# One pass for bias and maximum, zero-padded queries, and a searched order of the attention work

## Chip, cores and metric

The kernel runs on one core of a Trainium2 chip. The metric is the device time of one execution, in microseconds (us), as the median of three runs. All engine names are those of the profile: PE is the matrix engine, DVE, ACT and POOL are the vector, scalar and GpSimd engines, SP issues most DMAs.

## The reference

Two transformer layers act on 384 tokens: 256 latent tokens (a grid of 4 rows by 64 columns) and 128 context tokens. A layer normalises and modulates the tokens, projects them with one matrix, runs three kinds of attention on column groups of the result, concatenates their outputs, projects them, and adds a gated feed-forward network. All data are float32. The attention that the change touches is the neighbourhood kind, with 6 heads of width 64:

```
s_win = einsum('bhrqd,bhrjkd->bhrqjk', qg, kg) * scale + bias     # all 4 grid rows
s_win = where(in_win, s_win, NEG)                                 # 16 columns around the query
s_ctx = einsum('bhrqd,bhcd->bhrqc', qg, k_ctx) * scale            # 128 cached context keys
p = softmax(concatenate([s_win, s_ctx]))
o = p_win @ v + p_ctx @ v_ctx
```

The others are latent attention (MLA, 6 heads with keys of width 96) and differential attention (4 heads, the difference of two softmax maps). Context tokens attend to context tokens alone, in all three kinds.

## The kernel before

Tokens are handled in three tiles of 128 (two latent, one context). Every large product is split into a high and a low float32r part, so each product of 128 rows is three matmuls (`mm3`, lines 321 to 323). The weights arrive by DMA in `raw`, ACT rounds them to `wh` (line 254), and DVE forms the rest `wl` (line 260).

A layer has three stages. First comes the input projection, cut into 72 units of six matmuls (`g1`, tiles `z<-wh,hh`). I call them dense units, since PE can run them back to back. Second is attention, in pieces that are interleaved with the dense units. Third are the output projection and the feed-forward network. The output projection has 8 output blocks `m` of 8 units (three matmuls each, tiles `z<-oxh,wh` and `z<-o,wh`); the first three blocks are begun inside the attention stage.

The order of everything in the first two stages is made by a planner (`Plan`) when the program is built. Each piece is a task with an engine, a length in us, a priority, predecessors and the buffers it takes. `Plan.order` simulates the engines, always starts the ready task of lowest priority value, and lists the tasks by their simulated start. The program is recorded in that order, so every engine has one fixed queue. The planner halves PE's speed in windows that follow a thinly filled one. From the fourth output block on, the tile scheduler places instructions.

A softmax piece (`soft`) is: scores on PE (`score`, line 1037), the negated maximum on DVE (`maxima`, 1045), exponentials on ACT (`exps`, 1056), reciprocal and scaling on DVE (`norm`, 1061 and 1066), transposes of the weights on PE (`blocks_T`, 1004), and their copy on ACT (1106). `pair` makes four such pieces of 128 latent queries by 384 keys (two heads, two tiles), one piece for the context tokens, and the product with the values (1139, 1142). Neighbourhood pairs are made by `near(0)`, `near(1)` and `near(2)`, differential heads by `diff(0)` to `diff(3)`; `ORDER` lists in which sequence their priorities rise.

Before the change the two heads of a neighbourhood pair lie in partitions 0 to 63 and 64 to 127 of one tile, so a score matmul has 64 rows. The bias of 256 latent keys is added in place (line 1100) before the maximum is taken over 384. The bias tile has 6 x 64 columns. Normalised queries and keys come out of PE transposes (line 1209); ACT copies the queries (1212), DVE the keys (1215). `done_n` holds these steps.

Of the kernel before, what the change touches and what calls it, by code (L numbers as in the profile page):

```python
# [11 lines left out]
F32 = mybir.dt.float32  # L12
F32R = mybir.dt.float32r
AF = mybir.ActivationFunctionType
ALU = mybir.AluOpType
# [35 lines left out]
WARMUP = (18, 0.43, 16)  # L51
CYCLE = 'zszstzt'
# [5 lines left out]
HOPS = {('pe', 'act'): 0.2, ('pe', 'dve'): 0.16, ('act', 'pe'): 0.22, ('dve', 'pe'): 0.27, ('pool', 'dve'): 0.06, ('act', 'dve'): 0.15, ('dve', 'act'): 0.15}  # L58
# [23 lines left out]
class Plan:  # L82
# [8 lines left out]
    def add(self, eng, dur, fn, after=(), take=(), frees=(), prio=0.0, ready=0.0):  # L91
        t = Task(eng, dur, fn, take, prio, ready, LAG if eng == 'dma' else 0.0)
        self.tasks.append(t)
        for a in after:
            if a is not None:
                a.then.append(t)
                t.need += 1
        for h in frees:
            h.users += 1
            t.frees.append(h)  # L100
        return t

# [80 lines left out]
def trunk(ctx: ExitStack, tc, xT_d, cv_d, crow_d, pcol_d, prow_d, cache_d, dfk_d, rope_d, bias_d, ident_d,  # L183
# [378 lines left out]
    def parameters(l, staged=None):  # L562
# [14 lines left out]
        naq, lam, nlam, subg = (par.tile([P, 1], F32, tag=t, name=nm(t)) for t in ("naq", "lam", "nlam", "subg"))  # L577
# [7 lines left out]
        def gains():  # L585
            nc.vector.tensor_scalar(prow[:, PR_DQ:PR_DQ + 32], prow[:, PR_DQ:PR_DQ + 32], 32.0 ** -0.5, None, op0=ALU.mult)
            nc.vector.tensor_scalar(naq, pc[:, PC_NAQ:PC_NAQ + 1], 0.125, None, op0=ALU.mult)
# [25 lines left out]
    for l in range(DEPTH):  # L613
# [177 lines left out]
        def g1(ci, done, kbs=(0, 2, 4, 6), kind="z"):  # L791
# [3 lines left out]
            for kb in kbs:  # L795
# [3 lines left out]
                for t in range(3):  # L799
# [7 lines left out]
                    u = add(PE, 6 * (n / 2400 + 0.003), unit, after=[lo, last[t], hready[kb], hready[kb + 1]],  # L807
# [95 lines left out]
        def up_q(t, pr):  # L903
# [37 lines left out]
            p = add(POOL, 1.6, lambda: rsqrt(x["rs"], x["ms"], 96 * EPS), after=red, prio=pr)  # L941
# [5 lines left out]
        def up_kv(i, pr):  # L947
# [34 lines left out]
            p = add(POOL, 1.6, lambda: rsqrt(x["rs"], x["ms"], mskr[:, i:i + 1]), after=red, prio=pr)  # L982
# [38 lines left out]
        def soft(maps, after, spread, bias=None, joint=None, keep=None):  # L1021
# [18 lines left out]
            def maxima():  # L1040
                if bias:
                    bias(x["b"][0][0])
                x["mx"], i = small(n), 0
# [4 lines left out]
            def exps():  # L1048
                x["su"], x["e"] = small(n), []
                for ps, c in x["b"]:  # L1050
                    for j in range(c):
                        i = len(x["e"])
                        if nk == NT or i == 0:
# [3 lines left out]
                                             accum_out=x["su"][:, i:i + 1])  # L1057
# [14 lines left out]
            a = add(PE, COST_S * w / NT * (0.25 if joint else 1), score, after=after, take=("s",) * banks, prio=pr + PRS)  # L1072
            b = add(DVE, 0.08 * banks + 1.05e-3 * w + (0.34 if bias else 0), maxima, after=[a], prio=pr + PRM)
# [11 lines left out]
        def pair(kt, qk, v, h0, biased, after, vals, late=None):  # L1085
# [3 lines left out]
            for i in range(2) if biased else ():  # L1089
                def fetch(i=i):  # L1090
                    p["bias", i] = wk.tile([P, 6, 64], F32, tag="bias", name=nm("bias"))
                    nc.sync.dma_start(p["bias", i], bias_d[l, :, h0 + i])
                ld[i] = add(DMA, 0.3, fetch, take=("bias",), prio=seq[0])
                in_line("bias", ld[i])
            vs, scored, rooms = [], [], []
            for i in range(2):
                for t in range(2):
                    def bias(ps, i=i, t=t):
                        u0 = 2 - 2 * t
                        nc.vector.tensor_tensor(ps[:, 0, P:NT], ps[:, 0, P:NT],  # L1100
                                                p["bias", i][:, u0:u0 + 4, :].rearrange("p u c -> p (u c)"), op=ALU.add)
# [15 lines left out]
                    else:  # L1117
# [4 lines left out]

            x, a, e, pr = soft(lambda: [(qk()[0][i][:, NL:NT], qk()[1][i][:, NT:512], i == 0 or biased) for i in range(2)], after,
                               (P, 2, 2 if biased else 1), keep="pd")
# [44 lines left out]
        nu, na_ready, na_room = [], [[] for _ in range(3)], []  # L1169
        vn, vn_ready = [], [[] for _ in range(3)]  # L1170

        def na_units():
            nu.extend(units(3, P))
            dma.dma_start(nu[1][:, :, 0:P], cache_d[l, :, CA_NAK:CA_NAK + 384].rearrange("p (a b) -> p a b", a=3))

        def done_n(j):
            hd = slice(2 * j, 2 * j + 2)

            def done(t, z, unit, room):
# [6 lines left out]
                def vals():  # L1186
                    if j < 2 and t == 0:

                        vn.append(ws.tile([P, 4, 2 + 2 * j, 64], F32, tag="v" if j else "v0", name=f"vn{l}{j}"))
                        dma.dma_start(vn[j][:, 0].rearrange("p h d -> p (h d)"),  # L1190
                                      cache_d[l, :, CA_NAV + P * j:CA_NAV + P * j + P * (1 + j)])
                    v = vn[min(j, 1)][:, :, slice(0, 2) if j < 2 else slice(2, 4)]
# [18 lines left out]
                def queries():  # L1211
                    nc.scalar.activation(nu[0][:, j, t * P:(t + 1) * P], x["pt"][:, 0], AF.Copy, scale=naq)
# [16 lines left out]
                na_ready[j].append(add(ACT, 0.26, queries, after=[f], frees=[f], prio=pr))  # L1229
# [4 lines left out]
        dfo, vd, df_ready, vd_ready = [], [], [{}, {}], [[], []]  # L1234

        def done_d(p):
            hd = slice(2 * p, 2 * p + 2)

            def done(t, z, unit, room):
# [18 lines left out]
                def rotate():  # L1258
                    if t == 0:
                        dfo.append(ws.tile([P, 3, 8, 32], F32, name=nm("dfo")))  # L1260
# [24 lines left out]
                d = add(POOL, 1.9, lambda: rsqrt(x["rs"], x["ms"], EPS), after=[c], prio=pr)  # L1285
                e = add(DVE, 0.33, lambda: nc.vector.tensor_tensor(heads(x["n"], 8), heads(x["n"], 8), bc3(x["rs"], 32), op=ALU.mult),
                        after=[d], prio=pr)
                df_ready[p][t] = add(DVE, 1.25 if t < 2 else 0.34, rotate, after=[e], frees=[a], prio=pr)
# [4 lines left out]
        def df_unit(h, after, pr):  # L1293
# [19 lines left out]
            for t in range(3):  # L1313
# [29 lines left out]
                d = add(POOL, 0.86, parts_lo, after=[c], prio=pr)  # L1343
                e = add(PE, 0.37, stack, after=[d], take=("t",), frees=[c], prio=pr)
# [7 lines left out]
        def diff_step(h, t, st, after, late=()):  # L1352
# [30 lines left out]
            o = add(PE, 0.6 if t < 2 else 0.16, out, after=[v] + vd_ready[h // 2], take=("t",), frees=[x["room"]], prio=pr + PRO)  # L1383
# [3 lines left out]
        def diff_tail(h, st, late, pr):  # L1387
# [23 lines left out]
            c = add(POOL, 1.0, lambda: rsqrt(st["rs"], st["ms"], EPS), after=[b], prio=pr)  # L1411
# [41 lines left out]
        def near(j):  # L1453
            if not dense:
                dense.extend(t for t in plan.tasks if t.dense)
            sl = [slice(64 * i, 64 * i + 64) for i in range(2)]
# [277 lines left out]
```

## Time and profile before

| what | value |
|---|---|
| median of three runs | 1035.77 us (1035.76 to 1036.49) |
| the profiled execution, its own time | 1036.13 us |
| its span in the trace | 1034.4 us |
| PE busy | 1012.3 us, 98% |
| DVE, ACT, POOL busy | 719.5, 509.1, 172.7 us |
| layer 0: first score, last value product ends, output projection ends | 98.7, 213.9, 245.4 us |
| layer 1: the same | 598.7, 723.4, 749.4 us |

The span runs from the first to the last instruction; 1.7 us of the execution lie around it. "PE busy" counts a matmul until its modelled end, so neighbours overlap and a busy PE may still be waiting between starts. The starts of successive rows of the timeline tell its pace. "PEld" is the loading of weights, and "PEclk" the share of the full clock that PE was granted.

### The profile page before, as it was taken

How to read it: one execution, taken by the hardware profiler on the slowest of the kernel's cores; microseconds unless marked ns; L12 is line 12 of the kernel's file. 1: busy time of each engine (PE TensorE's matmuls, PEld its weight loads, DVE VectorE, ACT ScalarE, POOL GpSimd, SP SyncE). 2: the span in 40 equal slices, each digit the busy share in tenths (PEclk: the TensorE clock that was granted, in tenths of full speed). 3: DMA queues.
4: the chain of work that ended last, by engine and by line, in shares of the span. 5: the costliest groups of instructions: out<-in, count | busy, mean ns of one | idle time of the engine just before them, and what ended most of it. 6: DMA issues, size and time to landing. Idle time of an engine off the chain costs nothing.

```text
span 1034.4 us, 16528 instructions
## 1 busy us (share of the span) xinstructions
PE 1012.3 (98%) x6074; PEld 933.0 (90%) x6074; DVE 719.5 (70%) x1599; ACT 509.1 (49%) x1180; POOL 172.7 (17%) x263
## 2 busy tenths in 40 slices
PE   8999999989999999999999999989999999999998
PEld 7877779679999999999978878867999999999998
DVE  5677787955999999963455887766869755554332
ACT  3466778745433333343326668766653334333221
POOL 2266223201001001100024533230010000000000
PEclk9999999989999999999999999969999999999999
DMA  9865444125575757684463232410376434343441
GB/s 356 331 202 190 161 153 138 58 82 202 165 243 185 233 177 232 206 273 131 123 226 101 81 125 71 154 54 9 123 249 199 125 120 137 108 123 111 139 137 42
DMA packets 129681, 162.25 MB, mean 157 GB/s; under 512 B 5056, under 2 KB 111680, under 8 KB 127296
## 3 DMA queue, kind: packets, MB, share of 16 engines
q1 hardware_dynamic: 121184, 132.76, 40.3%
q0 software_dynamic: 6832, 27.77, 7.7%
q8 instruction: 48, 0.79, 0.3%
q10 hardware_dynamic: 1584, 0.66, 0.2%
q14 instruction: 33, 0.27, 0.1%
HBM read 158.12 MB, written 3.05 MB: 156 GB/s over the span
## 4 chain that ended last, share of the span: by engine, by line
PE 76%; DVE 2%; ACT 1%; POOL 1%; issue 1%; ACTq 0%; DVEq 0%; POOLq 0%
PE z L321 11%; PE z L323 11%; PE z L322 11%; PE t L322 6%; PE t L321 6%; PE t L323 6%; PE s L322 5%; PE s L323 5%; PE s L321 5%; PE s L1037 2%; PE t L1004 2%; PE t L1139 1%; POOL small L542 1%; PE t L1376 1%; PE z L1037 1%
## 5 line engine op out<-in xcount | busy, mean ns | idle before, releaser
L254 ACT ACTIVATE wh<-raw 128x1024 fp32r<-128x1024 f32 (+2 forms) x216 | 201.5, 934 | 366.0 <-PE z L322 138.8
L260 DVE TENSOR_TENSOR wl<-raw,wh 128x1024 fp32r<-128x1024 f32 (+2 forms) x216 | 230.7, 1070 | 111.6 <-ACT wh L254 111.2
L321 PE MATMUL z<-fh,wh 128*128 128x386 f32 x304 | 103.2, 339 | 0.0
L322 PE MATMUL z<-fl,wh 128*128 128x386 f32 x304 | 103.0, 339 | 0.0
L323 PE MATMUL z<-fh,wl 128*128 128x386 f32 x304 | 102.6, 338 | 0.0
L444 DVE CUSTOM_DVE_ANT_0 sums<-wt,sums,pcol 128x1024 f32<-128x1024 f32 x80 | 102.2, 1278 | 0.3 <-DVE small L1578 0.3
L321 PE MATMUL z<-wh,hh 128*128 128x384 f32 (+1 forms) x264 | 99.9, 379 | 1.1 <-ACT hh L514 0.5
L323 PE MATMUL z<-wh,hl 128*128 128x384 f32 (+1 forms) x264 | 90.3, 342 | 0.5 <-DVE hl L522 0.5
L322 PE MATMUL z<-wl,hh 128*128 128x384 f32 (+1 forms) x264 | 89.8, 340 | 0.0
L542 POOL TENSOR_TENSOR small<-small,mhalf 128x4 f32<-128x4 f32 (+4 forms) x58 | 73.2, 1262 | 4.8
L321 PE MATMUL s<-fh,wh 128*128 128x386 f32 x200 | 68.2, 341 | 0.0
L321 PE MATMUL t<-fh,wh 128*128 128x386 f32 x200 | 68.1, 340 | 0.0
L322 PE MATMUL t<-fl,wh 128*128 128x386 f32 x200 | 67.8, 339 | 0.0
L322 PE MATMUL s<-fl,wh 128*128 128x386 f32 x200 | 67.8, 339 | 0.0
L323 PE MATMUL t<-fh,wl 128*128 128x386 f32 x200 | 67.5, 338 | 0.0
L323 PE MATMUL s<-fh,wl 128*128 128x386 f32 x200 | 67.5, 338 | 0.0
L438 POOL DMA_DIRECT2D wt<-in_w_modT x40 | 21.5, 539 | 273.7 <-DVE mod L444 190.8
L321 PEld LDWEIGHTS z<-wh,hh 128*128 128x128 f32 x264 | 49.8, 189 | 9.2 <-issue 4.2
L322 PEld LDWEIGHTS z<-fl,wh 128*128 128x128 f32 x304 | 57.5, 189 | 0.0
L323 PEld LDWEIGHTS z<-fh,wl 128*128 128x128 f32 x304 | 57.3, 188 | 0.0
L321 PEld LDWEIGHTS z<-fh,wh 128*128 128x128 f32 x304 | 57.2, 188 | 0.0
L1056 ACT ACTIVATE e<-s,small 128x384 f32<-128x384 f32 (+1 forms) x102 | 51.0, 506 | 12.2 <-DVE small L1045 11.2
(316 smaller groups left out, 2422.8 us busy)
## 6 DMA issues: line engine op xcount, KB each, us to landing
raw<-in_w_gate SPq DMA_DIRECT2D x22, 1024.0 KB, 6.0
raw<-in_w_up SPq DMA_DIRECT2D x22, 1024.0 KB, 5.4
raw<-in_w_down SPq DMA_DIRECT2D x32, 704.0 KB, 4.8
wt<-in_w_modT POOLq DMA_DIRECT2D x40, 512.0 KB, 4.3
raw<-in_w_mod SPq DMA_DIRECT2D x16, 1024.0 KB, 5.0
raw<-in_w_in SPq DMA_DIRECT2D x40, 384.0 KB, 3.9
raw<-in_w_out SPq DMA_DIRECT2D x8, 1024.0 KB, 5.5
qu<-in_w_mod SPq DMA_DIRECT2D x8, 512.0 KB, 7.4
```

The source lines that it names most:

```text
L254: nc.scalar.activation(hi, src, AF.Copy)
L260: nc.vector.tensor_tensor(lo, src, hi.bitcast(F32), op=ALU.subtract)
L321: nc.tensor.matmul(out, sh, mh, start=first, stop=False)
L322: nc.tensor.matmul(out, sh, ml, start=False, stop=False)
L323: nc.tensor.matmul(out, sl, mh, start=False, stop=last)
L438: nc.gpsimd.dma_start(self.w[:, self.loaded % 3], w_modT[l, c * P:(c + 1) * P])
L444: nc.vector.tensor_tensor_reduce(self.junk, self.w[:, self.n % 3], self.s[:, v], 1.0, pcol[l][:, PC_BMOD + c:PC_BMOD + c + 1], ALU.mult, A ...
L542: nc.gpsimd.tensor_tensor(out, t[:, :n], mhalf[:, :n], op=ALU.pow)
L1004: nc.tensor.transpose(pt[:, b, :], x, ident)
L1037: nc.tensor.matmul(ps[:, i, :], q, k, start=True, stop=True)
L1056: nc.scalar.activation(x["e"][i], ps[:, j, :], AF.Exp, bias=x["mx"][:, i:i + 1], accum_out=x["su"][:, i:i + 1])
L1139: nc.tensor.matmul(po[64 * i:64 * i + 64, 0:NL], vv[:, b, v0 + i, :], p["pT"][i][:, b, :], start=(b == 0), stop=(b == 2), tile_position=(0 ...
```

## The change

Neighbourhood scores: each head's query tile now has 128 rows, with zeros in the other head's 64 (the two columns of `naq` hold the gain in one half and zero in the other). ACT therefore writes two query copies for each transpose, and the score matmul uses the whole key tile. There are four query tiles, so pair 2 reuses those of pair 0, and the turning of pair 2 waits for the scores of pair 0. The two context maps now share one PSUM bank and one reduction.

Bias and maximum: one `tensor_tensor_reduce` over all 384 keys adds the bias, negates, and keeps the minimum; the exponential gets `scale=-1`. The bias tile grows to 5 x 128 columns (zeros for the context keys), the DMA from 0.20 to 0.33 MB for each of 12 loads.

Order: several task lengths and hand-over times are set anew, and `Plan.best` runs the planner 300 more times with a seeded random change of some priorities, keeping the shortest simulated order. This happens while the program is built. Tiles that were made by the first pair in program order are now made by whichever comes first.

```diff
+ORDERS, STIR = 300, 3.0
...
+    def best(self):
...
+        draw = random.Random(0)
+        base = [t.prio for t in tasks]
+        free = [i for i, t in enumerate(tasks) if t.dur and t.eng != "room"]
+        best = list(base)
+        run(best)
+        end = self.end
+        for _ in range(ORDERS):
+            p = list(best)
+            for i in draw.sample(free, draw.choice((1, 2, 4, 8, 16, 40))):
+                p[i] = base[i] + draw.gauss(0, STIR if draw.random() < 0.8 else 5 * STIR)
+            try:
+                run(p)
+            except AssertionError:
+                continue
+            if self.end <= end:
+                end, best = self.end, p
+        return run(best)
...
-HOPS = {('pe', 'act'): 0.2, ('pe', 'dve'): 0.16, ...}
+HOPS = {('pe', 'act'): 0.22, ('pe', 'dve'): 0.22, ..., ('dve', 'pool'): 0.18, ...}
-u = add(PE, 6 * (n / 2400 + 0.003), unit, ...)
+u = add(PE, 6 * (n / 2400 + 0.0135), unit, ...)
-p = add(POOL, 1.6, lambda: rsqrt(...), ...)
+p = add(POOL, 2.1, lambda: rsqrt(...), ...)
...
 def maxima():
+    x["mx"], i = small(n), 0
     if bias:
-        bias(x["b"][0][0])
-    x["mx"], i = small(n), 0
+        s = x["b"][0][0][:, 0, :]
+        s = s.rearrange("p (b k) -> p b k", k=P)
+        nc.vector.tensor_tensor_reduce(s, s, bias(), -1.0, 3e38, ALU.add, ALU.min, x["mx"])
+        return
...
-p["bias", i] = wk.tile([P, 6, 64], F32, tag="bias", name=nm("bias"))
+p["bias", i] = wk.tile([P, 5, P], F32, tag="bias", name=nm("bias"))
-x, a, e, pr = soft(... i == 0 or biased) for i in range(2)], after, (P, 2, 2 if biased else 1), keep="pd")
+x, a, e, pr = soft(... i == 0) for i in range(2)], after, (P, 2, 1), keep="pd")
...
 def queries():
-    nc.scalar.activation(nu[0][:, j, t * P:(t + 1) * P], x["pt"][:, 0], AF.Copy, scale=naq)
+    for i in range(2):
+        nc.scalar.activation(nu[0][(2 * j + i) % 4][:, t * P:(t + 1) * P], x["pt"][:, 0], AF.Copy, scale=naq[:, i:i + 1])
...
-work = plan.order()
+work = plan.best()
```

The order moves on every engine. Three places follow, each as the program before has it and then as the changed one has it.

PE in layer 1, from just after the last dense unit (`z<-wh,hh`). Lines 1037 and 1073 are the scores, 1004 and 1040 the transposes, 1376 and 1420 the value products of differential attention, 1209 and 1250 the turning of neighbourhood queries and keys, 1335 the stacking of differential queries and keys; `ku_7098` is the last differential head, `ku_7112` and `ku_6845` the neighbourhood keys.

```order
L1004 MATMUL t_7761<-ident,e_7709 128x128
L1376 MATMUL t_7768<-vd_6337,pd_7749 128x64 x3
L1037 MATMUL z_7778<-ku_7098,qu_7097 128x128 x2
L1376 MATMUL t_7793<-vd_6337,pd_7781 128x64
L1209 MATMUL t_7799<-ident,tok_7720 128x128 x2
L1037 MATMUL s_7806<-ku_7112,qu_7111 128x128
L1037 MATMUL s_7808<-ku_7112,qu_7111 128x128
L1209 MATMUL t_7823<-ident,tok_7736 128x128 x2
L1037 MATMUL z_7835<-ku_7112,qu_7111 128x384
L1004 MATMUL t_7843<-ident,e_7789 128x128 x3
L1209 MATMUL t_7859<-ident,tok_7763 128x128 x2
L1037 MATMUL z_7862<-ku_7112,qu_7111 128x384
```

```order
L1040 MATMUL t_7978<-ident,dn_7351 128x128 x3
L1040 MATMUL t_7989<-ident,e_7932 128x128 x3
L1073 MATMUL z_7999<-ku_6845,qu_6844 128x384
L1073 MATMUL z_8007<-ku_6845,qn_6846 128x384
L1073 MATMUL z_8017<-ku_6845,qn_6846 128x384
L1420 MATMUL t_8031<-vd_6345,pd_8019 128x64 x3
L1250 MATMUL t_8037<-ident,tok_7943 128x128 x2
L1073 MATMUL s_8046<-ku_6845,qu_6844 128x128
L1073 MATMUL s_8046<-ku_6845,qn_6846 128x128
L1250 MATMUL z_8050<-ident,tok_7951 128x128 x2
L1250 MATMUL t_8063<-ident,tok_7985 128x128 x2
L352 MATMUL z_8070<-oxh_5867,wh_7898 128x384
```

What follows the last dense unit before is the rest of two differential heads and all three neighbourhood pairs: 24 score rows, 45 transposes and 12 stackings up to the last value product. Now it is the rest of pair 1 and pair 2: 11 score rows, 32 transposes and no stacking, with output units (line 352) reached sooner. In layer 0 the scores fall from 20 to 10 and the transposes from 38 to 28. The dense units that stand behind the first score rise from 31 to 36 in layer 0 and from 33 to 40 in layer 1; the output units left after the last value product rise from 47 to 52 and from 49 to 51.

DVE in layer 0, from the end of attention into the output projection. `xT<-z` (534, 565) adds a finished output block, `fl` (529, 560) prepares the feed-forward input, `sq` (464, 495) sums squares, and the `wl` of line 260 or 291 is the low part that output block 3 needs.

```order
L1551 TENSOR_TENSOR fl_3058<-mod_101,fh_3057 128x8x2
L534 SCALAR_TENSOR_TENSOR xT<-z_2741,mod_101,xT 128x256
L534 SCALAR_TENSOR_TENSOR xT<-z_2741,mod_101,xT 128x128
L534 SCALAR_TENSOR_TENSOR xT<-z_2791,mod_101,xT 128x256
L534 SCALAR_TENSOR_TENSOR xT<-z_2791,mod_101,xT 128x128
L534 SCALAR_TENSOR_TENSOR xT<-z_2986,mod_101,xT 128x256
L534 SCALAR_TENSOR_TENSOR xT<-z_2986,mod_101,xT 128x128
L529 SCALAR_TENSOR_TENSOR fl_3058<-xT,aff_103,fh_3057 128x256
L529 SCALAR_TENSOR_TENSOR fl_3058<-xT,aff_103,fh_3057 128x128
L529 SCALAR_TENSOR_TENSOR fl_3058<-xT,aff_103,fh_3057 128x256
L464 TENSOR_TENSOR sq_3039<-sq_3039,sq_3043 128x384
L260 TENSOR_TENSOR wl_3048<-raw_2342,wh_3030 128x1024
```

```order
L1598 TENSOR_TENSOR fl_3052<-mod_101,fh_3051 128x8x2
L565 SCALAR_TENSOR_TENSOR xT<-z_2779,mod_101,xT 128x256
L565 SCALAR_TENSOR_TENSOR xT<-z_2779,mod_101,xT 128x128
L291 TENSOR_TENSOR wl_3021<-raw_2574,wh_3009 128x1024
L560 SCALAR_TENSOR_TENSOR fl_3052<-xT,aff_103,fh_3051 128x256
L560 SCALAR_TENSOR_TENSOR fl_3052<-xT,aff_103,fh_3051 128x128
```

The low part stood behind ten instructions, the last of which sums squares that ACT makes; now it stands behind the update of one block.

DVE again, at a neighbourhood piece late in layer 0: 1061 and 1101 are reciprocals, 1066 and 1106 the scaling, 1100 the bias, 1045 the maximum, 1082 the joint instruction, whose second row reads out the accumulated value.

```order
L1061 RECIPROCAL small_2916<-small_2894 128x1
L1066 TENSOR_SCALAR e_2895<-e_2895,small_2916 128x384
L1100 TENSOR_TENSOR z_2887<-z_2887,bias_2833 128x256
L1045 TENSOR_REDUCE small_2925<-z_2887 128x1
L1061 RECIPROCAL small_2927<-small_2921 128x1
```

```order
L1082 ISA z_2866,small_2903<-z_2866,bias_2794 128x384
L1082 ISA small_2903 128x1
L1101 RECIPROCAL small_2910<-small_2891 128x1
L1106 TENSOR_SCALAR e_2892<-e_2892,small_2910 128x384
L1085 TENSOR_REDUCE small_2913<-s_2875 128x2
```

Two instructions over 256 and 384 elements have become one over 384 and a readout, and the two context maps are reduced by one instruction (1085).

More of the change, by code (lines that the diff above doesn't have):

```diff
@@ L2 @@
 import math
+import random
 from contextlib import ExitStack
@@ L101, in add, with run @@
         return t
+    def best(self):
+        tasks, room, dense = self.tasks, dict(self.room), self.dense
+        was = [(t.need, t.users, t.ready) for t in tasks]
+        def run(prios):
+            for t, (t.need, t.users, t.ready), t.prio in zip(tasks, was, prios):
+                t.held = []
+            self.room, self.dense = dict(room), dense
+            return self.order()
+        draw = random.Random(0)
[15 more added lines that the diff above has]
+        return run(best)
     def fit(self, t):
@@ L806, in unit @@
                                 kb + k == 0, kb + k == KD - 1)
-                    u = add(PE, 6 * (n / 2400 + 0.003), unit, after=[lo, last[t], hready[kb], hready[kb + 1]],
+                    u = add(PE, 6 * (n / 2400 + 0.0135), unit, after=[lo, last[t], hready[kb], hready[kb + 1]],
                             take=((kind[t] if len(kind) > 1 else kind),) if kb == 0 else (), frees=[hi], prio=DENSE)
@@ L1071, in soft @@
             w = n * nk
-            a = add(PE, COST_S * w / NT * (0.25 if joint else 1), score, after=after, take=("s",) * banks, prio=pr + PRS)
-            b = add(DVE, 0.08 * banks + 1.05e-3 * w + (0.34 if bias else 0), maxima, after=[a], prio=pr + PRM)
+            a = add(PE, (0.22 if joint else COST_S) * w / NT, score, after=after, take=("s",) * banks, prio=pr + PRS)
+            b = add(DVE, 0.08 * banks + 1.05e-3 * w + (0.06 if bias else 0), maxima, after=[a], prio=pr + PRM)
             c = add(ACT, n * 0.25 + 0.85e-3 * w, exps, after=[b], take=("e",) * (n if nk == NT else 1), frees=[a], prio=pr + PRX)
@@ L1097, in pair, with bias @@
                 for t in range(2):
[L1098 to L1101, printed above, removed]
+                    def bias(i=i, t=t):
+                        return p["bias", i][:, 0:3] if t else p["bias", i][:, 0:5:2]
                     def evac(x, i=i, t=t):
@@ L1643, in _bias_index @@
     idx = dr[:, :, None] * 31 + rc[:, None, :]
-    return np.where(inw[:, None, :], idx, 15 * 31)
+    idx = np.where(inw[:, None, :], idx, 15 * 31)
+    out = np.full((P, 5, P), 15 * 31 + 1)
+    for b, u in ((1, 0), (2, 2), (4, 4)):
+        out[:, b] = idx[:, u:u + 2].reshape(P, P)
+    return out
 def _rope_table():
```

72 lines of the change are left out of this document (42 added, 30 removed).

## Prediction

> **What bounds the kernel now.** I read the page first, for the engines, the clock and the chain of waits that ended last.
>
> ```profile
> span 1034.4 us, 16528 instructions
> PE 1012.3 (98%) x6074; PEld 933.0 (90%) x6074; DVE 719.5 (70%) x1599; ACT 509.1 (49%) x1180; POOL 172.7 (17%) x263
> PE   8999999989999999999999999989999999999998
> PEclk9999999989999999999999999969999999999999
> PE 76%; DVE 2%; ACT 1%; POOL 1%; issue 1%; ACTq 0%; DVEq 0%; POOLq 0%
> ```
>
> PE carries the end: 98% busy and most of the chain. In two places its clock was not full, in slices 9 and 27, where the attention stages end. The view by windows (core's busy time per engine, granted clock, DMA) then divides the two layers at the same events. A layer's rows are: before the first score (layer 1), first score to last dense unit, from there to the last value product, and the output projection. The row 678.30:698.80 lies inside the one above it.
>
> ```profile
> core 0: us, PE busy (x) PEld busy (x) DVE busy (x) ACT busy (x) POOL busy (x), PEclk, DMA share, GB/s
> 98.70:180.10 81.40, 80.49 (x552) 65.80 (x552) 64.68 (x172) 63.41 (x209) 24.50 (x45) 1.00 0.50 159
> 180.10:213.90 33.80, 32.54 (x206) 23.77 (x204) 26.53 (x81) 23.57 (x76) 6.75 (x10) 1.00 0.16 48
> 213.90:245.40 31.50, 27.83 (x143) 26.61 (x142) 21.68 (x43) 15.53 (x30) 0.00 (x0) 0.89 0.32 100
> 535.90:598.70 62.80, 59.82 (x326) 54.36 (x327) 46.29 (x119) 39.92 (x110) 36.71 (x48) 1.00 0.37 119
> 598.70:674.20 75.50, 74.10 (x461) 61.81 (x460) 59.90 (x155) 56.53 (x178) 22.97 (x38) 1.00 0.36 108
> 674.20:723.40 49.20, 46.10 (x238) 32.72 (x236) 33.94 (x98) 31.82 (x108) 10.90 (x19) 0.79 0.10 32
> 678.30:698.80 20.50, 19.01 (x61) 11.92 (x63) 13.62 (x41) 12.14 (x43) 5.84 (x11) 0.50 0.05 14
> 723.40:749.40 26.00, 26.00 (x149) 25.88 (x149) 21.01 (x43) 15.77 (x30) 0.00 (x0) 1.00 0.40 122
> ```
>
> The last row is PE at its pace: 149 matmuls in 26.00 us, 0.1745 us each, weight loads without a gap. So a dense unit (six) is 1.05 us, an output unit (three) 0.52. Two losses stand out. Layer 1 spent 20.5 us at half clock, 19.0 of them busy. Layer 0 took 31.5 us for the 47 output units after its last value product, where layer 1 needed 26.0 for 49.
>
> PE's timeline shows how the clock was lost: the three waits (in brackets) just before 678.3 are short.
>
> ```profile
> 676.02 0.43 PE L1376 MATMUL t<-vd,pd 128*128 128x64 f32 x2 [0.38 <-ACT pd L1370]
> 676.73 0.41 PE L1209 MATMUL t<-ident,tok 128*128 128x128 f32 x2 [0.28 <-ACT e L1056]
> 678.62 0.66 PE L1209 MATMUL t<-ident,tok 128*128 128x128 f32 x2 [0.79 <-ACT e L1056]
> ```
>
> No long idle stretch precedes the drop. The dense units had ended and short matmuls were left, each waiting for ACT or DVE; the half clock then held for 20.5 us of such work. The Trainium skill (TensorE: Matmul & The Clock Gate, Part 1) puts the drop after one idle window of about 3.4 us and the return after one busy window. By that rule no drop was due here, and a drop would cost some 1.7 us instead of 9.5; the trace differs on both, so I follow the rows.
>
> **The change part by part.** *Layer 1's end of attention.* After the last dense unit 24 score rows become 11, stacking goes, and the two differential heads' leftovers and pair 0 lie among dense units instead. What is left resembles layer 0 before (20 scores, 38 transposes), whose 33.8 us ran at clock 1.00. If the clock holds, half of 19.0 busy us is saved, 9.5. A second estimate compares layers: first score to end of projection is 150.7 us in layer 1 and 146.7 in layer 0. Layer 0 contains the stall priced next (6.9) and four more blocks of modulation matmuls; layer 1 contains two more dense units (2.1).
>
> ```profile
> 142.44 1.07 PE L372 MATMUL m<-raw,sv 128*32 128x256 f32 x16
> 143.44 0.91 PE L1037 MATMUL s<-ku,qu 64*128 64x384 f32 x2
> ```
>
> Such a block is 1.0 us from start to start, so layer 0's pace gives layer 1 146.7 - 6.9 - 4.0 + 2.1 = 137.9, and 12.8 are lost. I take -10, near the half-clock row, which is the direct one; ends 0 (the clock is lost again) and -12.8.
>
> *Layer 0's entry into the projection.* PE, then DVE and ACT:
>
> ```profile
> 218.73 0.45 PE L321 MATMUL s<-oxh,wh 128*128 128x384 f32 x1 [0.32 <-ACT wh L254]
> 220.08 0.45 PE L321 MATMUL z<-oxh,wh 128*128 128x384 f32 x1 [0.72 <-ACT wh L254]
> 223.32 0.69 PE L323 MATMUL z<-oxh,wl 128*128 128x384 f32 x1 [2.62 <-DVE wl L260]
> 223.81 0.52 PE L321 MATMUL z<-oxh,wh 128*128 128x384 f32 x1
> ```
>
> ```profile
> 216.67 2.01 ACT L254 ACTIVATE wh<-raw 128x1024 fp32r<-128x1024 f32 x2 [2.05 <-PE z L322]
> 221.57 0.56 DVE L464 TENSOR_TENSOR sq<-sq,sq 128x384 f32<-128x384 f32 x1
> 222.05 3.49 DVE L260 TENSOR_TENSOR wl<-raw,wh 128x1024 fp32r<-128x1024 f32 x3
> ```
>
> The high part was there by 217.7, the low part was queued on DVE until 222.05. PE waited, and the next matmuls ran slow (0.52 against 0.34 us long). Now the low part is third after the first block's update, about 219 on this scale. Also 12 output units, 6.3 us, are left after the last value product instead of 7, so PE has work until the part arrives. The lost time is 31.5 - 47 x 0.52 = 6.9. I take -6.5; ends 0 and -6.9. Layer 1's projection already runs at pace: 0. Late next would be block 4's low part, two DVE parts later, while PE does 4.2 us of block 3; so it stays hidden.
>
> *Neighbourhood pieces, 24 latent and 6 context.* PE's timeline, score rows and the rows after them:
>
> ```profile
> 187.66 1.55 PE L1037 MATMUL z<-ku,qu 64*128 64x384 f32 x4
> 189.21 0.55 PE L1004 MATMUL t<-ident,e 128*128 128x128 f32 x3
> ...
> 110.95 0.81 PE L1037 MATMUL s<-ku,qu 96*128 96x384 f32 x2
> 111.60 0.38 PE L1004 MATMUL t<-ident,e 128*128 128x128 f32 x2
> ...
> 197.61 0.49 PE L1037 MATMUL s<-ku,qu 64*128 64x128 f32 x4
> 198.03 0.55 PE L1004 MATMUL t<-ident,e 128*128 128x128 f32 x3
> ...
> 128.28 0.61 PE L1037 MATMUL s<-ku,qu 96*128 96x128 f32 x4
> 128.72 0.45 PE L1376 MATMUL t<-vd,pd 128*128 128x64 f32 x3
> ```
>
> Two 64-row maps take 1.55 us, 0.775 each; a 96-row map takes 0.65. The nearest row for 128 rows is 96, so 24 x 0.125 = 3.0 us leave PE. The context's two maps take 0.42 with 64 rows and 0.44 with 96: nothing. The Trainium skill (TensorE: Matmul & The Clock Gate, Part 3) says that matmuls in different row groups overlap, which full rows give up. If the two context maps had gained a factor of two that way, six pieces at 0.42 would cost 2.5 us more and the sum would be 1018; the 96-row maps show no such gap.
>
> DVE and ACT, groups by form, and the bias load's DMA:
>
> ```profile
> L1100 DVE TENSOR_TENSOR s<-s,bias 128x256 f32<-128x256 f32 x17 | 7.2, 426 | 1.4 <-PE s L1037 1.2
> L1045 DVE TENSOR_REDUCE small<-s 128x1 f32<-128x384 f32 x67 | 35.7, 552 | 4.6 <-PE s L1037 3.7
> L444 DVE CUSTOM_DVE_ANT_0 sums<-wt,sums,pcol 128x1024 f32<-128x1024 f32 x80 | 102.2, 1278 | 0.3 <-DVE small L1578 0.3
> L444 DVE DVE_READ_ACCUMULATOR2_ANT mod<- 128x1 f32 x80 | 6.6, 82 | 0.0
> L1212 ACT ACTIVATE qu<-t,naq 128x128 f32<-128x128 f32 x17 | 6.0, 367 | 3.8 <-PE t L1209 2.8 <-ACT vn L1193 0.4 <-DVE ku L1215 0.4
> DMA to landing us min/median/max: 2.2/3.1/10.3
> ```
>
> Bias and maximum cost 0.426 + 0.552 = 0.98 us. The joint instruction is known only on 1024 elements of SBUF: 1278 x 384/1024 + 82 is 0.56; as slow as the two it replaces is 0.98. I take 552 + 82 = 0.63, the row with the same elements in the same memory; DVE gains 24 x 0.35 = 8.3 us (ends 0 and 10). ACT gets 18 more query copies, 6.6 us. Neither is PE's bound; they shorten and lengthen the same chains, and between them I count -0.5 (ends +3 and -4). Together -3.5, ends 0 and -7. The bias transfers are issued ahead and land in 3.1 us; 0.13 MB more in each hides behind the pair before it. Where that cover goes, the next pair's four scores wait. The new wait of pair 2's turning for pair 0's scores is on PE itself, which reaches the turning after those scores anyway: 0.
>
> *The rest of the order.* First scores now stand five dense units earlier in layer 0 and seven in layer 1, and ACT, DVE, POOL and SP are reordered with them: modulation loads, cache and bias loads on SP, the roots on POOL. PE's total of work is unchanged by that. What it waits more or less, no row of before can show. Bounds: -10 (a third of the 29.3 us by which weight loads fall short of the window in the rows 98.70:180.10 and 598.70:674.20) and +12.6 (the twelve units' 1.05 us all uncovered). I take 0, since the same kind of interleaving stands on both sides.
>
> Sum, on the profiled execution's 1036.1 (the median of the runs is 0.4 under it): -10 - 6.5 - 3.5 = -20, so 1016; for the median as well, within rounding.
>
> **The rivals.**
> *The clock is lost again in one of the ends.* The ends now have 28 and 32 transposes with 12 and 13 output units, where they had 17 and 15. For it: three waits of under 0.8 us were enough at 676. Against it: layer 0's end held 1.00 with 38. One stretch like that of before gives back 9.5: 1026. The Trainium skill (TensorE: Matmul & The Clock Gate, Part 4) says that transposes do not count as busy for the clock, which would make thin ends of this kind lose it; layer 0's end before does not bear it out.
> *The order gains more.* The ends of the other waits come too, the -10 above: 1006. For it: weight loads fill only 65.80 of 81.40 us there. Against it: nothing says that PE's chains shorten.
> *It does not do what it says.* The lengths do not hold on the chip, and PE meets new waits that eat the 20: 1034 to 1038.
> *Slower.* The scores come too early for the up-projections, whose chain goes through POOL and DVE (36.71 and 46.29 busy of 62.80 us before the first score). PE then has up to 12.6 us less cover there, and if its clock drops in both layers as at 678, another 2 x 9.5 go: 1016 + 12.6 + 19 = 1048. It is slower than before from the point where both clocks drop and 3 us of the cover are lost. Against it: PE was 59.82 of 62.80 busy there.
>
> **How the numbers follow.** Forecast, 1010 to 1021: 0.50. Clock lost again, 1022 to 1031: 0.21. More gained, 1001 to 1009: 0.14. No gain: 0.07. Slower: 0.08. From 1003 to 1031 holds about 0.8: the forecast, the clock rival, and two thirds of the better one. A change under 0.2% (2 us) is about what cannot be told from none. Faster takes the first three and a little of the fourth, 0.87; same 0.05; slower 0.08.
>
> **What would show it.** Clock 1.00 in layer 1's end, and no DVE `wl` wait on PE in layer 0's projection, which then takes some 0.52 us per unit. The joint instruction at 0.5 to 0.7 us, scores with 128 rows at 0.65. The prediction is wrong if a half-clock stretch stands anywhere in the attention stages, or if the time from the first dense unit to the first score does not fall with the five and seven units taken from it.

## The result, and the profile after

The changed kernel takes 1013.54 us (median of 4 runs, 1012.24 to 1013.70) against 1036.13 for the kernel before beside it (4 runs, 1035.76 to 1037.82): a ratio of 0.9776, 95% interval 0.9759 to 0.9793, or 22.6 us less. The forecast was 1016, range 1003 to 1031. The profiled run took 1013.45 us, with a span of 1011.7.

The page of the changed kernel, the same lines as those shown of before:

```profile
span 1011.7 us, 16532 instructions
PE 996.6 (99%) x6074; PEld 927.7 (92%) x6074; DVE 710.8 (70%) x1597; ACT 510.3 (50%) x1198; POOL 171.7 (17%) x263
PE   8999999999999999999999999999999999999998
PEclk9999999999999999999999999999999999999999
```

PE is still the bound, with 15.7 us less of busy time for the same 6074 matmuls. No slice shows a lowered clock any more. To see where the time went, both kernels are cut at the same events: first dense unit of layer 0, end of its output projection, first dense unit of layer 1, end of its projection. First before, then after, in the view by windows (busy time and count of PE, PEld, DVE, ACT, POOL; granted clock; DMA share; GB/s):

```profile
21.00:245.40 224.40, 217.23 (x1450) 176.80 (x1445) 167.69 (x462) 147.10 (x433) 68.50 (x98) 0.98 0.50 165
245.40:535.90 290.50, 289.39 (x1663) 283.81 (x1661) 223.38 (x417) 109.38 (x162) 23.18 (x42) 1.00 0.63 203
535.90:749.40 213.50, 206.03 (x1168) 174.76 (x1169) 161.14 (x413) 144.05 (x424) 70.58 (x103) 0.95 0.31 96
```

```profile
20.90:237.40 216.50, 211.85 (x1449) 176.07 (x1446) 163.71 (x463) 148.00 (x442) 65.44 (x98) 1.00 0.52 174
237.40:529.20 291.80, 290.86 (x1661) 283.95 (x1659) 223.46 (x417) 109.21 (x162) 23.15 (x42) 0.99 0.63 203
529.20:726.70 197.50, 193.75 (x1168) 169.59 (x1169) 156.37 (x410) 144.42 (x433) 72.61 (x103) 1.00 0.34 106
```

Layer 0's stretch gave 7.9 us and layer 1's 16.0; the stretch between them took 1.3 more. What lies behind layer 1's projection is unchanged: 280.9 us in both, up to PE's last matmul. The stages of the changed kernel, cut as in the prediction (layer 0: first score to last dense unit, to the last value product, projection; layer 1: before the first score, then the same three; last, the end of the stretch between the layers):

```profile
93.10:188.80 95.70, 93.69 (x642) 76.67 (x642) 75.52 (x211) 72.98 (x242) 28.16 (x48) 1.00 0.48 154
188.80:209.80 21.00, 20.04 (x132) 15.62 (x130) 15.18 (x54) 15.87 (x51) 4.24 (x7) 1.00 0.19 60
209.80:237.40 27.60, 27.60 (x159) 27.60 (x158) 21.39 (x43) 15.77 (x30) 0.00 (x0) 1.00 0.36 115
529.20:582.60 53.40, 52.53 (x283) 46.73 (x284) 41.93 (x108) 35.68 (x101) 34.58 (x45) 1.00 0.32 103
582.60:675.00 92.40, 91.37 (x589) 78.16 (x588) 74.54 (x201) 74.57 (x245) 32.47 (x50) 1.00 0.36 113
675.00:699.70 24.70, 22.85 (x147) 17.70 (x145) 18.69 (x61) 18.39 (x58) 5.57 (x9) 1.00 0.24 73
699.70:726.70 27.00, 27.00 (x156) 27.00 (x155) 21.20 (x43) 15.78 (x30) 0.00 (x0) 1.00 0.38 118
522.00:526.00 4.00, 4.00 (x19) 0.96 (x18) 0.84 (x4) 0.00 (x0) 0.87 (x1) 0.57 0.53 167
```

Both ends of attention are short now: 21.0 and 24.7 us after the last dense unit, where 33.8 and 49.2 stood, because more dense units are left to lie among the scores. Layer 0's projection is 27.60 busy of 27.60 us for 52 units (0.53 each, 0.67 before). The last row holds a new stretch of half clock. It is 3.4 us long and lies shortly before layer 1's first dense unit, and the 1.3 us go with it: every run below whose trace lacks it takes 290.2 to 290.5 us between the layers.

DVE's and PE's timelines at the entry into layer 0's projection show the wait gone:

```profile
212.72 0.74 DVE L565 SCALAR_TENSOR_TENSOR xT<-z,mod,xT 128x256 f32<-128x256 f32 x2 [1.67 <-PE z L354]
213.64 1.23 DVE L291 TENSOR_TENSOR wl<-raw,wh 128x1024 fp32r<-128x1024 f32 x1 [0.17 <-ACT wh L285]
...
209.45 0.39 PE L1179 MATMUL t<-pd,vn 128*64 128x128 f32 x4
209.77 0.45 PE L352 MATMUL z<-o,wh 128*128 128x384 f32 x1
210.06 0.34 PE L353 MATMUL z<-o,wh 128*128 128x384 f32 x1
210.23 0.34 PE L354 MATMUL z<-o,wl 128*128 128x384 f32 x1
```

The low part starts 3.8 us after the last value product (8.1 before), and PE still has output units of the blocks before it. The neighbourhood's instructions, by groups (joint instruction under two names, its readout) and PE's timeline (128-row scores with the row after each):

```profile
L1082 DVE CUSTOM_DVE_ANT_1 s<-s,bias 128x384 f32<-128x384 f32 x10 | 5.7, 567 | 0.1
L1082 DVE CUSTOM_DVE_ANT_0 s<-s,bias 128x384 f32<-128x384 f32 x8 | 4.6, 569 | 0.0
L1082 DVE DVE_READ_ACCUMULATOR2_ANT small<- 128x1 f32 x24 | 3.4, 142 | 0.0
...
189.52 0.86 PE L1073 MATMUL s<-ku,qn 128*128 128x384 f32 x2
190.22 0.49 PE L1040 MATMUL z<-ident,e 128*128 128x128 f32 x3
190.55 0.81 PE L1073 MATMUL s<-ku,qn 128*128 128x384 f32 x2
191.19 0.38 PE L1250 MATMUL t<-ident,tok 128*128 128x128 f32 x2
...
199.97 0.61 PE L1073 MATMUL s<-ku,qu 128*128 128x128 f32 x4
200.34 0.42 PE L352 MATMUL z<-o,wh 128*128 128x384 f32 x1
```

A map takes 0.70 and 0.64 us from start to start, the context's two 0.37 together (0.42 before). Bias and maximum take 0.567 + 0.142 = 0.71 us.

### The profile page after: what moved, and what is told of

It is laid out like the page before. It is cut to its first block, busy times and chain, and to the rows that moved or that the text cites. A ratio compares the mean times of both kernels' runs of the same rounds, so it can differ in the third digit from the quotient of the medians.

```text
span 1011.7 us, 16532 instructions
## 1 busy us (share of the span) xinstructions
PE 996.6 (99%) x6074; PEld 927.7 (92%) x6074; DVE 710.8 (70%) x1597; ACT 510.3 (50%) x1198; POOL 171.7 (17%) x263
## 5 line engine op out<-in xcount | busy, mean ns | idle before, releaser
L573 POOL TENSOR_TENSOR small<-small,mhalf 128x4 f32<-128x4 f32 (+4 forms) x58 | 72.2, 1245 | 4.8
L1096 ACT ACTIVATE e<-s,small 128x384 f32<-128x384 f32 (+1 forms) x112 | 56.3, 511 | 11.4 <-DVE small L1085 8.2
```

What stands on the lines that cost most here:

```text
L573: nc.gpsimd.tensor_tensor(out, t[:, :n], mhalf[:, :n], op=ALU.pow)
L1096: nc.scalar.activation(x["e"][i], ps[:, j, :], AF.Exp, bias=x["mx"][:, i:i + 1], scale=-1.0 if bias else 1.0, accum_out=x["su"][:, i:i + 1])
```

## The experiments

Each edit is against the changed kernel or the kernel before, as said. The table gives every run: its median, its ratio to the kernel before on the same chip with 95% interval, and from its profiled execution the three stretches of above. The kernel before took 1036.86 us on the chip of e1 to e4, 1036.08 on that of e5 to e8 and 1037.59 on that of e9, e10, g1 and g2, so two rows from different chips are better compared by their ratios.

| run | median us | ratio | layer 0 | between | layer 1 |
|---|---|---|---|---|---|
| before | 1036.13 | 1 | 224.4 | 290.5 | 213.5 |
| changed | 1013.54 | 0.9776 [0.9759, 0.9793] | 216.5 | 291.8 | 197.5 |
| e1 no search | 1024.02 | 0.9885 [0.9868, 0.9901] | 222.0 | 290.4 | 203.4 |
| e2 old pieces, searched | 1027.56 | 0.9918 [0.9899, 0.9937] | 225.1 | 290.5 | 204.1 |
| e3 pieces alone | 1031.18 | 0.9954 [0.9936, 0.9971] | 227.6 | 290.4 | 205.2 |
| e4 filled waits | 1033.12 | 0.9970 [0.9959, 0.9981] | 224.7 | 290.4 | 210.0 |
| e8 the same, narrower | 1031.86 | 0.9961 [0.9947, 0.9974] | 224.3 | 290.4 | 209.6 |
| e9 fewer | 1032.50 | 0.9951 [0.9936, 0.9966] | 224.2 | 290.4 | 210.7 |
| e10 low part early | 1031.86 | 0.9952 [0.9936, 0.9967] | 218.1 | 290.4 | 213.8 |
| e5 bias apart | 1019.88 | 0.9843 [0.9829, 0.9856] | 219.4 | 290.4 | 201.9 |
| e6 64 rows | 1016.10 | 0.9810 [0.9796, 0.9824] | 217.7 | 291.8 | 199.5 |
| e7 other seed | 1016.09 | 0.9804 [0.9791, 0.9818] | 215.0 | 291.9 | 200.5 |
| g1 longer search | 1013.06 | 0.9767 [0.9754, 0.9781] | 216.1 | 290.2 | 197.5 |
| g2 and true lengths | 1014.39 | 0.9781 [0.9763, 0.9799] | 215.4 | 291.7 | 199.1 |

My theory was that the order brings the gain, by the clock in layer 1 and the low part in layer 0; the rival, that the cheaper pieces bring it. The first three runs take the change apart.

**e1: no search.** Edit to the changed kernel:

```
-ORDERS, STIR = 300, 3.0
+ORDERS, STIR = 0, 3.0
```

> The changed kernel with its new pieces and new lengths, but one planned order in each layer and no search among 300. Theory (most of the gain is the order that the search found: the work left for layer 1's end of attention keeps the clock full, and the first output block's low part comes early): about half of the 22.6 us goes, so 1024 us, between 1019 and 1031, and a stretch of half clock or a wait for a low part stands again in one of the layers. Rival (the corrected lengths alone give this order's worth, the search adds little): 1013 to 1016. Rival (the cheaper neighbourhood pieces bring the gain, whatever the order): 1013 to 1016 as well, told apart by the next two.

1024.02 us. About half of the gain goes with the search, 5.5 us in layer 0 and 5.9 in layer 1. A stretch of half clock of 3.4 us stands in each layer, in layer 0 in the end of attention, in layer 1 among the last dense units (the clock column of two windows there):

```profile
196.00:206.00 10.00, 7.49 (x42) 4.87 (x43) 8.89 (x28) 6.86 (x23) 1.54 (x2) 0.83 0.32 105
665.00:680.00 15.00, 12.69 (x73) 11.30 (x72) 9.14 (x22) 10.48 (x37) 6.83 (x14) 0.89 0.26 77
```

At most 1.7 us each, so the half clock is not the larger part of the 5.5 and 5.9: in the first row PE is idle for 2.5 of 10 us, in the second for 2.3 of 15. Pieces and lengths together gave the other half.

**e2: the old pieces, with new lengths and search.** The kernel before with `plan.best()` and the new lengths; scores with 64 rows, bias and maximum apart, one query copy.

> The kernel before with the new lengths and the search alone: neighbourhood scores with 64 rows, the bias added by itself, one query copy. Theory (order): the 3.5 us of the pieces are lacking, 1017 us, between 1014 and 1021, and no half clock in layer 1's end. Rival (pieces bring the gain): 1028 to 1036. Rival (the search's result is luck that another set of lengths does not repeat): a half-clock stretch comes back, 1023 to 1031.

1027.56: the theory's 1017 is missed by 10 us. Layer 1 kept 9.4 of its 16.0 us, although 6.8 us of half clock stand in its end; layer 0 kept nothing of its gain. Layer 0's projection (window), and PE's timeline in it:

```profile
215.20:246.30 31.10, 27.43 (x141) 26.22 (x140) 21.66 (x43) 15.53 (x30) 0.00 (x0) 0.89 0.32 102
...
224.08 0.69 PE L354 MATMUL z<-oxh,wl 128*128 128x384 f32 x1 [2.63 <-DVE wl L291]
```

The low part of block 3 comes late exactly as before: 31.1 us for 46 units, 7 lost. So a search does not bring it forward by itself: the plan holds the first three output blocks and the fourth's low part, but not the fourth's matmuls, so that their wait is not in the end that the search shortens. In e1 and e3, with the new pieces and no search, PE has no such wait. The early low part of the changed kernel thus goes with the order that the new pieces bring; the search does not aim at it.

**e3: the new pieces alone**, with the old lengths and no search.

> The kernel before with the new neighbourhood pieces alone: full rows, joint bias and maximum, two query copies, and lengths of their own; all other lengths as before and no search. Theory (order): -3.5 us, 1032.5, between 1029 and 1036; the half clock in layer 1's end and the late low part in layer 0's projection are still there. Rival (pieces bring the gain): 1020 or less, without the half clock. Rival (the pieces give nothing, since PE's chains do not shorten by what PE saves): 1036.

1031.18, near the number but not by its reasons. Cheaper pieces made the planner order everything anew: layer 1 lost its half clock and 8.3 us, layer 0 took 3.2 us longer. There the projection runs at pace (29.2 us, 55 units), but the clock is at half for 6.8 us in its end of attention, and for 6.8 us more among the dense units before (0.51 in the first row). The rows are that window, layer 0's end and projection, and the whole of layer 1:

```profile
176.50:183.40 6.90, 6.15 (x21) 6.06 (x22) 2.71 (x7) 4.96 (x22) 2.94 (x6) 0.51 0.00 0
185.70:219.60 33.90, 30.16 (x179) 23.13 (x178) 26.46 (x85) 26.01 (x86) 6.52 (x11) 0.90 0.18 56
219.60:248.80 29.20, 29.20 (x168) 29.17 (x167) 21.48 (x43) 15.86 (x30) 0.00 (x0) 1.00 0.33 108
539.20:744.40 205.20, 195.94 (x1168) 170.05 (x1169) 156.22 (x410) 145.42 (x433) 69.48 (x103) 1.00 0.33 104
```

The parts cannot be added up, then: each changes the order for the others. What one part is worth by itself has to be measured in a fixed order, as the next runs do.

**e4, e8, e9: the half clock of layer 1, by itself.** The kernel before, its order untouched; added matmuls stand where the plan has PE waiting between the last dense unit and the last value product. e8 has them 64 columns wide, e9 has 23 in place of 42.

```
 t.fn(...)
+for _ in range(extra.get(id(t), 0)):
+    nc.tensor.matmul(fill[0][:, 0:P], ident, ones, start=True, stop=True)
```

> The kernel before, word for word in its order, with 42 matmuls of 128x128 (0.11 us each, 4.5 us in all, into a bank that nothing else uses by then; their results are read by nobody) put into PE's waits in layer 1's end of attention. Theory (the half clock costs 9.5 us there): the clock stays at 1.00 and the kernel gains 9.5 less what the added matmuls hold up, 1027.5 us, between 1025 and 1031. Rival (the half clock only goes along with the waits, and the chains through ACT and DVE set the pace): the clock stays full but PE waits that much longer, 1035 to 1038. Third way: the added matmuls do not keep the clock, 1036 to 1040.

> As the run with filled waits, but each of the 42 added matmuls is 128x64. There each 128x128 one stood as two records of 0.11 us, 9.0 us in all, and PE had no wait left (45.62 us busy of 45.70), so its 3.7 us of gain were what the clock gave less what the additions took. Here they are 4.5 us. Theory (the half clock costs 9.5): full clock, 1028 to 1031. Rival (ACT's and DVE's chains set the pace, and the half clock filled waits that would be there anyway): full clock, 1032.5 to 1034.5, with PE waiting in this stretch again. Third way: the clock drops again, 1035 to 1038.

> The kernel before in its order with 23 added 128x128 matmuls (46 records of 0.11 us, 5.1 us in all, about the size of the waits) in place of 42. In the two runs with 42 PE was busy through the whole end of layer 1's attention (45.87 of 46.00 us), with 9 us of it added work, so those bound what the half clock cost there only between 3.5 and 12.5 us. Theory (it cost 9.5): full clock and the time from the last dense unit to the last value product, 49.2 us before, at 42 or less: 1026 to 1030 us. Rival (ACT's and DVE's chains set the pace, the half clock took the place of waits): full clock, and PE waits again; 45 us or more there, 1031 to 1034. Third way: too few, the clock drops again, 1035 to 1038.

1033.12, 1031.86 and 1032.50. My sizes were wrong twice: a 128x128 one is two records, and the narrow ones start no closer together (e8: ten records in 1.12 us, the row after them at 678.86). So e4 and e8 carry 84 records, 9.2 us. From the last dense unit to the last value product, e4, e8 and e9, and an extract of e8's timeline:

```profile
674.50:720.20 45.70, 45.62 (x323) 36.82 (x321) 34.07 (x98) 31.71 (x108) 11.16 (x19) 1.00 0.11 35
...
675.60:720.90 45.30, 45.17 (x322) 36.69 (x320) 33.66 (x98) 31.54 (x108) 11.11 (x18) 1.00 0.11 35
...
675.80:722.20 46.40, 45.74 (x285) 34.41 (x283) 33.80 (x98) 31.59 (x108) 10.95 (x19) 0.93 0.11 35
...
677.74 1.28 PE L1537 MATMUL fill<-ones,ident 128*128 128x64 f32 x10
678.86 0.39 PE L1209 MATMUL t<-ident,tok 128*128 128x128 f32 x2
```

The added work keeps the clock at 1.00 in e4 and e8, so the half clock did follow from thin work on PE. With 5.1 us in e9, two windows of 3.4 us still drop. What the half clock cost is only bounded. It cost at least 3.9 us (49.2 to e8's 45.3, additions paid for). The other bound is argued: of e8's 45.17 busy us, 36.0 are the kernel's own work, and before had 3.1 us of idle time in the same stretch; if faster matmuls do not make that less, 39.1 us is the least to be expected, so it cost at most 10.1. (The expectation of e9 took e8's end as 46.00 us; that window was cut at the times of the kernel before, and e8 runs 1.4 us later.)

The five runs of e9 give a hint on what lies between. From the slowest to the fastest the mean clock rises from 0.991 to 0.996 and the time falls from 1035.0 to 1030.56 us. Over their spans that is 18.6 and 8.2 us of half clock, so 4.4 us of time for 10.4 us, 0.43 each. At this rate the 20.5 us of the kernel before would cost 8.8 us. The nine runs of the kernel before on that chip give 0.36 when a line is laid through them, so 7.5 us. Both are estimates, since only the profiled runs show where the windows lay. Neither theory nor rival is excluded by this; it stays open.

**e10: the low part of layer 0, by itself.** The kernel before, with one DVE task moved:

```
 work = plan.order()
+if l == 0:
+    low = max(..., key=work.index)
+    work.remove(low)
+    work.insert(work.index(first) + 1, low)
```

> The kernel before with one thing moved: DVE makes the low part of output block 3 of layer 0 right after the first block's update, not after three updates and the norm's squares. Theory (PE waits at the projection's entry for this part alone, and the half clock behind it goes with the wait): the projection after the last value product falls from 31.5 us to between 24.6 and 25.5 for the same 47 units, 1029.5 us, between 1028 and 1031. Rival (the next low part, or the updates that are now behind it, is late instead): 1033 to 1037.

1031.86, ratio 0.9952. The projection (first row; the second is DVE's timeline, where the low part now starts right after the first update):

```profile
213.60:239.30 25.70, 25.38 (x143) 24.79 (x142) 21.11 (x43) 15.80 (x30) 0.00 (x0) 1.00 0.39 123
...
217.46 1.23 DVE L260 TENSOR_TENSOR wl<-raw,wh 128x1024 fp32r<-128x1024 f32 x1 [0.17 <-ACT wh L254]
```

31.5 has become 25.7 us for the same 47 units, and the half clock behind the wait is gone with it. The other stretches stand as before. This part is shown: 5.8 us by the trace, and 3.4 to 6.6 by the interval of the ratio. The profiled run is the fastest of the five (1030.24 us, mean clock 0.990); the others have 0.986 to 0.988, so 4 to 8 us more of half clock in places that no trace shows.

**e5 and e6: the pieces' prices in the changed kernel's own order.** PE's order is that of the changed kernel. e5 adds the bias and takes the maximum apart; e6 takes 64 rows, the head's own (`h`), in the 24 latent scores.

```
-nc.vector.tensor_tensor_reduce(s, s, bias(), -1.0, 3e38, ALU.add, ALU.min, x["mx"])
+nc.vector.tensor_tensor(s, s, bias(), op=ALU.add)
+nc.vector.tensor_reduce(x["mx"], x["b"][0][0], axis=AX.X, op=ALU.max, negate=True)
...
-nc.scalar.activation(..., scale=-1.0 if bias else 1.0, accum_out=...)
+nc.scalar.activation(..., accum_out=...)
```

```
-[(qk()[0][i][:, t * P:(t + 1) * P], qk()[1][i][:, 0:NT], True)]
+[(qk()[0][i][h, t * P:(t + 1) * P], qk()[1][i][h, 0:NT], True)]
```

> The changed kernel in its own order, instruction for instruction, but for the 24 maxima of the neighbourhood's latent queries: the bias is added by one instruction (384 wide, 0.43 to 0.65 us) and the maximum taken by another (0.55), in place of the joint one (0.57 and 0.14 us). Theory (the pieces' own price is small; what the run of the old pieces with a search, 1027.6, lacks besides is its order): DVE does some 7 us more off PE's path, 1015 us, between 1013.5 and 1018. Rival (the cheaper pieces themselves carry the 14 us between that run and the changed kernel): this and the next run together are 10 us or more above 1013.5, so 1019 or more here.

> The changed kernel in its own order, but the 24 latent score matmuls of the neighbourhood pairs take 64 rows of query and key instead of 128 (the context's six keep 128). Theory (own price: 0.775 against 0.65 us a map): 24 x 0.125 = 3 us more on PE, 1016.5, between 1015 and 1019. Rival (the cheaper pieces carry the 14 us): 1019 or more here or in the run before. Rival (the rows cost nothing where PE waits anyway): 1013 to 1014.5.

e6 gives 1016.10: 2.6 us for the rows, beside the 3.0 foreseen. e5 gives 1019.88: 6.3 us, the rival's number. By the ratios it is 3.5 and 6.9 us; e6's interval begins just above the end of the changed kernel's (0.9796 and 0.9793), so its price is rough. Groups of e5 on DVE, two waits of PE in its layer 0 (in brackets), and its layer 1 from the last dense unit to the last value product:

```profile
L1082 DVE TENSOR_TENSOR s<-s,bias 128x384 f32<-128x384 f32 x18 | 10.0, 558 | 0.1
L1083 DVE TENSOR_REDUCE small<-s 128x1 f32<-128x384 f32 x18 | 10.0, 557 | 0.6
...
196.29 0.44 PE L1251 MATMUL t<-ident,tok 128*128 128x128 f32 x2 [0.61 <-DVE tok L1266]
206.65 0.52 PE L1040 MATMUL t<-ident,e 128*128 128x128 f32 x3 [0.81 <-DVE e L1107]
...
677.20:705.80 28.60, 26.00 (x147) 19.80 (x144) 22.79 (x61) 18.79 (x58) 5.39 (x9) 0.88 0.20 64
```

1.115 us against 0.71: 24 x 0.41 = 9.7 us on DVE, of which 6.3 came out at the end, although DVE is busy for 70% of the span. In layer 0's end PE now waits for two of DVE's results, 0.81 and 0.61 us, where the changed kernel has no wait for DVE; in layer 1's, 6.8 us of half clock come back, so that up to 3.4 of the 6.3 us can be the clock's. The addition is 384 wide here and 256 in the kernel before (0.43 us), so against before the joint instruction saves 0.27 us a map, two thirds of this; scaled so, an estimate, 4.2 us. With the rows 6.8 to 8.9 us are the pieces' own in a fixed order, if the two prices add up; no run has both. The rest of the 14 us between e2 and the changed kernel is about the size of e2's late low part (7), which is a sum and not a run.

**e7: another seed.** `random.Random(1)` in place of 0.

> The changed kernel with another seed of its search, all else the same. Theory (a search of 300 finds an order whose time on the chip spreads by several us, by whether a low part comes late or the clock drops for a stretch): somewhere between 1009 and 1024, more likely above 1013.5 than below, and a difference, if there is one, stands in one layer with a half-clock stretch or a late low part. Rival (the search finds much the same worth each time): 1011 to 1016.

1016.09, 2.5 us above. Layer 0 is 1.5 us shorter, layer 1 is 3.0 us longer. As the theory has it, a stretch of half clock stands in the longer layer; it lasts 3.4 us and lies ahead of that layer's first score (0.72 is the clock of a window around it):

```profile
538.00:544.00 6.00, 5.81 (x18) 4.22 (x19) 3.87 (x9) 2.63 (x8) 0.75 (x2) 0.72 0.34 99
```

That is at most 1.7 of the 3.0 us. The time is 0.1 us beyond the rival's range and well inside the theory's, and one more seed does not tell how wide the spread is.

**g1 and g2: more draws, truer lengths.** The changed kernel with the priorities that 2500 draws find; in g2 also `0.06` to `0.23` for bias and maximum and `0.53` to `0.68` for the query copies.

> The changed kernel with the order that the same search finds after 2500 draws instead of 300; by the planner's own lengths the two layers end 1.3 and 1.9 us earlier than in the changed kernel. Theory (the lengths hold on the chip to a per cent or so, so more draws still pay): 1008 to 1012 us. Rival (what is left is finer than the lengths, so the result spreads as between the two seeds, 1013.5 and 1016.1): 1012 to 1018, with a low part late or a stretch of half clock in it.

> As the run with 2500 draws, but the planner's length of the joint bias and maximum is raised from 0.54 to the measured 0.71 us, and that of the two query copies from 0.53 to 0.68 us. Theory (lengths that the trace shows make the better order): 1007 to 1011 us, no slower than the run with 2500 draws alone. Rival (the two lengths hardly matter beside the spread of orders): 1011 to 1018, on either side of that run.

1013.06 and 1014.39, both in the rivals' ranges. The planner's 1.3 and 1.9 us do not arrive: g1's layers are those of the changed kernel to 0.4 us (the two rows), with no stretch of half clock in either; g2's are 1.1 us shorter and 1.6 longer.

```profile
21.90:238.00 216.10, 212.12 (x1449) 176.34 (x1446) 164.44 (x463) 148.06 (x442) 64.93 (x98) 1.00 0.51 174
528.20:725.70 197.50, 193.30 (x1171) 170.02 (x1168) 156.07 (x410) 143.76 (x434) 72.08 (x103) 1.00 0.34 108
```

Nothing here beats the changed kernel: g1's interval covers its ratio.

## Why the prediction was right, and where its steps were not

The sum was 20 us and 22.6 came; by layers, 8.2 of layer 0 (6.5 and half of 3.5) and 11.8 of layer 1 were expected, and 7.9 and 16.0 came.

*Layer 0's entry (-6.5).* Right in place, reason and size. The same edit alone gives 5.8 us (e10), and the changed kernel has no wait there and 0.53 us a unit. The prediction saw that the matmuls behind the wait ran slow, but did not name the half clock; the clock of 0.89 stood in the row.

*Layer 1's end (-10).* The clock is 1.00, as forecast, and the end is 24.5 us shorter, with dense units moved up among its scores. But the step "if the clock holds, half of 19.0 busy us is saved, 9.5" took for the likely value one near the upper bound; the filled waits leave 3.9 to 10.1. Why it may be less is argued, not shown: slow matmuls cover waits that a full clock uncovers. About half of layer 1's 16.0 us came without the clock: e3, whose layer 1 has no half clock, is still 7.7 us from the changed kernel there.

*Neighbourhood pieces (-3.5).* Mis-sized. The rows were priced well (3.0, measured 2.6 in the fixed order). The step that fails is "Neither is PE's bound; they shorten and lengthen the same chains, and between them I count -0.5". The joint instruction takes 0.71, not 0.63 us, and was still worth 6.3 us against the 384-wide pair (about 4 against the one before). ACT makes 36 copies in place of 18, at 0.37 us each as before, yet its busy time rose by 1.2 us in all and not by 6.6; what the copies cost the kernel no run takes apart.

*The rest of the order (0).* Mis-sized too: the search gives 10.5 us in the changed kernel over its own lengths and pieces (e1), and e1 has no late low part and 6.8 us of half clock in all, 3.4 us at most of those 10.5. The row that the prediction gave for such a gain does not show it: among the dense units of layer 0 weight loads fill 80% of the time, as before (65.80 of 81.40 us, 76.67 of 95.70). From the first score to the last value product, the time without loads (window less PEld) went from 25.6 to 24.4 us in layer 0 and from 30.2 to 21.2 in layer 1, so it is in layer 1 that PE's work closed up.

So that the total came out this near is in part luck: a price of the half clock near the top of what the runs allow stood against two that were too low. *The rivals.* The clock was not lost in an end of the changed kernel, but that rival was close: in e1, e2, e3 and e5 it was, in stretches of 3.4 to 6.8 us, shorter and cheaper than the 9.5 assumed. A stretch of 3.4 us stood before layer 1's first dense unit instead, at 1.3 us. The cover of the up-projections was not lost: from first dense unit to first score 72.2 and 53.4 us, 5.4 and 9.4 less for five and seven units. Full rows in the context cost nothing that shows, so the 1018 that the prediction gives for a lost factor of two did not come.

## What to carry to other kernels

When several parts of a change pass through a planner, run each alone to learn what orders it brings, but price it in a fixed order: alone the pieces looked worth 5 us with all layers moved, in place they are worth some 7 to 9. An engine that is busy 70% of the time can still set the pace in a stage where every piece of work passes through it, so cost a shorter instruction there by the chain and not by the engine's share. Do not count half the busy time of a throttled stretch as the gain of curing it: fill its waits with idle work first, and see what is left.

## What was not expected of the hardware

The stretches of half clock inside the traces last 3.41, 6.83 or 20.48 us: one, two or six times 3.41. The Trainium skill (TensorE: Matmul & The Clock Gate, Part 1) has a free-running window of 3413 ns, and the lengths agree. Its return to full clock after one busy window does not: before, the clock stayed halved for six windows in which PE was busy for 19.0 of 20.5 us, by the profile's measure. Part 4 of that page of the Trainium skill says that transposes do not count as busy in the same way. No run here puts that to the test: the changed kernel's layer 1 end has 44 of them at clock 1.00 (38 of line 1040 and 6 of line 1250; the 32 counted ahead of the prediction are those of tile `e` alone, and the other three counts there lack 12 likewise), but among 40 output matmuls.

Whether a single window drops also differs from one execution to the next. In the profiled executions of the changed kernel, e6, e7 and g2 the window before layer 1's first dense unit is at half clock (291.7 to 291.9 us between the layers), in the ten others, before among them, it is not (290.2 to 290.5), with as many matmuls there (1661 to 1663). The profiled executions of e6, e8, e9 and g2 have such a window at 14 to 19 us as well. The times of one kernel's runs go along with the clock: g2's two runs at a mean clock of 1.000 took 1012.99 and 1013.16 us, its two at 0.997 took 1015.61 and 1016.45, the last with both of these windows in its trace.

A joint addition and minimum over 384 elements takes DVE 0.567 us where the addition alone takes 0.558; only the readout of 0.142 is added.
